# Attention by halves: when a head's second 256 queries may begin

## The chip, the cores and the metric

The kernel runs on one core of a Trainium2 chip. The metric is the time of one execution on the device, in microseconds (us). The core's engines work side by side, each through a list of its own, and wait for each other by semaphores: TensorE (PE, with its weight loads as PEld), VectorE (DVE), ScalarE (ACT), GpSimd (POOL) and SyncE (SP), which issues the DMA transfers.

## What is computed

One residual block over 1024 tokens of 1024 features, in float32. Cut to what matters:

```
h = x + 0.5 * g1 * swiglu(n1, w1, w3, w2)            # first FFN
proj = n2 @ w_in
y_rwkv = rwkv7_mixer(proj[..., :N_RWKV_COLS], ...)   # 8 heads, a recurrence
...
bias = rel_bias[:, rel_idx]                          # 8 heads of 64
scores = jnp.einsum('bhcqd,bhckd->bhcqk', q, k_band) * (HEAD_DIM ** -0.5)
scores = scores + bias[None, :, None]                # each 64 frames see themselves and 512 before
probs = jax.nn.softmax(scores, axis=-1)
out = jnp.einsum('bhcqk,bhckd->bhcqd', probs, v_band)
...
mixed = jnp.concatenate([y_rwkv, y_attn], axis=-1) @ w_out
h = h + g2 * mixed
h = h + 0.5 * g3 * swiglu(n3, ...)                   # second FFN
```

## The kernel before

The tokens are worked in two halves, A and B, of 512. Each half goes through first FFN, input projection, recurrence and attention, output projection and second FFN. The big products ("mm", or "mmb" where the result lies in one of the shared banks) keep float32 accuracy by splitting each operand into a high and a low part and multiplying three times: weights arrive as "wst", ScalarE makes the high part "whi" and VectorE the low part "wlo"; activations are "nh" and "nl", the FFN's hidden values "ah" and "al" (from "sw"), the mixed heads "mh" and "ml". Each such product has 128 rows of weights and streams 512 columns.

Everything is written as generators. A generator yields what it needs next: tiles that have to be ready, or the name of a pool in which a buffer has to be free. `drive` keeps a clock of estimated times for every engine and resumes the first task, in the order of priorities, whose needs the clock has ready; if there is none, it moves its clock to the earliest. So the program's order on every engine, fixed when the program is built, comes from these priorities and estimates. The big products come from one task of the lowest priority, `products`, and fill what the others leave. The FFN's two output stages of one token half can be interrupted by a projection only as `pick` allows: first FFN of A, projection of A, first FFN of B (which is begun before that projection and goes on behind it), output projection of A, projection of B, second FFN of A (into which the output projection of B is put as soon as the mixed heads of B are there), second FFN of B.

Attention has one pair of tasks for each of eight heads and each token half: `head_in` loads and splits keys, queries and values (K, QH, QL, V) and the bias, and `attention` does the rest, in two rounds of 256 queries (`for qp in range(2)`), each of two blocks of 128. For each block: scores S on TensorE (two products, QH and QL); VectorE adds the bias, writes E and its maximum; ScalarE takes the exponential and scales by the reciprocal sum; TensorE transposes E in blocks of 128 keys ("tr"); ScalarE copies the high part of the transposed probabilities ("pt") and VectorE subtracts to get the low part; TensorE multiplies both with the values ("yp"); ScalarE and VectorE add the two halves of yp into yT, which is stored when both rounds are done. There are 2 buffers for E, 6 in the pool "t2" (yT, pt, QH, QL and the loads), 2 for K and V, 1 for the bias, and 5 shared PSUM banks "b" (S, tr, yp, the recurrence's products and part of the big ones). A head's task starts when the task of the head before it has ended; so the next round's scores come behind the last yT of the round before.

The recurrence (`rwkv1`, `inverse`, `rwkv2`) runs at the same time. Its products are small ("px", "pu", "pz", "gb", "bt" and others); `inverse` is a long list of VectorE operations on "BKB" and "ln". "V" is the values' split.

Of the kernel before, what the change touches and what calls it, by code (L numbers as in the profile page):

```python
# [8 lines left out]
F32 = mybir.dt.float32  # L9
F32R = mybir.dt.float32r  # L10
AF = mybir.ActivationFunctionType
OP = mybir.AluOpType
# [4 lines left out]
P = 128  # L17
T = 1024
D = 1024
H = 512  # L20
# [8 lines left out]
NEG = -3.0e38  # L29
# [220 lines left out]
class Builder:  # L250
# [770 lines left out]
    def head_in(self, hf, hd, st):  # L1021
# [44 lines left out]
        yield vd  # L1066
        nc.scalar.activation(V[:, :, 0], vd, AF.Copy)
        yield V
        nc.vector.tensor_sub(V[:, :, 1], vd, V[:, :, 0].bitcast(F32))
        st["V"] = V  # L1070

    def attention(self, hf, hd, st):
        nc = self.nc
        p, h = hd // 2, hd % 2
        hs = slice(h * 64, h * 64 + 64)
        has = lambda k: lambda: self.clock.ready(st[k]) if k in st else NEVER
        yield has("QL"), has("bias")
        QH, QL, K, bias = (st[k] for k in ("QH", "QL", "K", "bias"))
        yield "t2"
        yT = self.t2("yT")  # L1080
        for qp in range(2):
            pr = []
            for i in range(2):
                b = 4 * hf + 2 * qp + i
                k0 = max(0, b - 4)
                n = (b - k0 + 1) * P
                q = (2 * qp + i) * P
                S = []

                m = n if n <= H else n // 2  # L1090
                for c0 in range(0, n, m):
                    yield QL, K, "b"
                    S.append((self.bank("S"), c0, m))
                    k = k0 * P + c0
                    self.mm(S[-1][0][:, 0:m], QH[:, q : q + P], K[:, k : k + m], start=True, stop=False)
                    self.mm(S[-1][0][:, 0:m], QL[:, q : q + P], K[:, k : k + m], start=False, stop=True)
                yield *(x[0] for x in S), "E"
                E = self.sm("E", [P, 640], 2)
                sm = self.sm("st", [P, 4], 4)
                for j, (x, c0, m) in enumerate(S):  # L1100
                    nc.vector.tensor_tensor_reduce(
                        out=E[:, c0 : c0 + m], in0=x[:, 0:m], in1=bias[:, 640 - n + c0 : 640 - n + c0 + m],
                        scale=1.0, scalar=NEG, op0=OP.add, op1=OP.max, accum_out=sm[:, 2 * j : 2 * j + 1],
                    )
                if n > H:
                    nc.vector.tensor_scalar(sm[:, 1:2], sm[:, 0:1], sm[:, 2:3], -1.0, OP.max, OP.mult)
                else:
                    nc.vector.tensor_scalar(sm[:, 1:2], sm[:, 0:1], -1.0, None, OP.mult)
                pr.append((b, k0, E, sm, n))
            if qp == 1:  # L1110
                self.free(K, QH, QL)
            for b, k0, E, sm, n in pr:
                yield sm
                nc.scalar.activation(E[:, 0:n], E[:, 0:n], AF.Exp, bias=sm[:, 1:2], accum_out=sm[:, 2:3])
            for b, k0, E, sm, n in pr:
                yield sm
                nc.vector.reciprocal(sm[:, 3:4], sm[:, 2:3])
            for b, k0, E, sm, n in pr:
                yield E, sm
                nc.scalar.activation(E[:, 0:n], E[:, 0:n], AF.Copy, scale=sm[:, 3:4])  # L1120
                self.free(sm)
            blocks = []
            for kb in range(pr[0][1], pr[1][0] + 1):
                blocks.append((kb, [i for i in range(2) if pr[i][1] <= kb <= pr[i][0]]))
            blocks.sort(key=lambda x: -len(x[1]))
            nb = len(blocks)
            trs, pts, yp = {}, {}, None
            span = lambda bi: slice(blocks[bi][1][0] * P, blocks[bi][1][-1] * P + P)
            for bi in range(nb + 2):
                if bi < nb:  # L1130
                    kb, use = blocks[bi]
                    yield *(pr[i][2] for i in use), "b"
                    trs[bi] = self.bank("tr", 2)
                    for i in use:
                        k0 = pr[i][1]
                        self.tp_(trs[bi][:, i * P : i * P + P], pr[i][2][:, (kb - k0) * P : (kb - k0 + 1) * P], self.ident)
                if bi == nb - 1:
                    self.free(pr[0][2], pr[1][2])
                if 1 <= bi <= nb:
                    yield pts[bi - 1]  # L1140
                    c = span(bi - 1)
                    nc.vector.tensor_sub(pts[bi - 1][:, 1, c], trs[bi - 1][:, c], pts[bi - 1][:, 0, c].bitcast(F32))
                if bi < nb:
                    yield trs[bi], "t2"
                    c = span(bi)
                    pts[bi] = self.t2("pt", [P, 2, 256], F32R)
                    nc.scalar.activation(pts[bi][:, 0, c], trs[bi][:, c], AF.Copy)
                if 1 <= bi <= nb:
                    yield pts[bi - 1], has("V"), *(["b"] if bi == 1 else [])
                    V = st["V"]  # L1150
                    if bi == 1:
                        yp = self.bank("yp", 2)
                    c = span(bi - 1)
                    lv = V[:, blocks[bi - 1][0]].rearrange("p a c -> p (a c)")
                    pt = pts.pop(bi - 1)
                    self.mm(yp[:, c], lv, pt[:, 0, c], start=bi == 1, stop=False, skip_group_check=True)
                    self.mm(yp[:, c], lv, pt[:, 1, c], start=False, stop=bi == nb, skip_group_check=True)
                    self.free(pt)
            q0 = qp * 256
            yield yp  # L1160
            nc.scalar.activation(yT[0:64, q0 : q0 + 256], yp[64:128, 0:256], AF.Copy)
            yield yT
            nc.vector.tensor_add(yT[0:64, q0 : q0 + 256], yT[0:64, q0 : q0 + 256], yp[0:64, 0:256])
# [588 lines left out]
```

## Time and profile before

| what | value |
|---|---|
| median of 3 runs | 2111.45 us (2110.54 to 2112.09) |
| the profiled execution, its own time | 2110.92 us |
| its span, from the first to the last instruction | 2109.0 us |
| TensorE busy | 2086.1 us, 99% of the span |
| VectorE busy | 1443.9 us, 68% |
| ScalarE busy | 946.7 us, 45% |
| GpSimd busy | 119.2 us, 6% |

The span is shorter than the execution's own time by what lies ahead of the first and behind the last instruction. Matrix products overlap each other in their records: each lasts longer than the distance to the next one's start, so TensorE's busy time says that it always has something in work, not how fast it starts the next. For that, read the starts in the timeline.

### The profile page before, as it was taken

To read this page: it belongs to the slowest core of one execution; us is meant where nothing else is said; L and a number is where in the kernel's file an instruction comes from. 1 tells how busy PE (TensorE), PEld (TensorE's weight loads), DVE (VectorE), ACT (ScalarE), POOL (GpSimd) and SP (SyncE) were. 2 spreads that over 40 slices of the span, in tenths; PEclk is the share of its full clock that TensorE was granted. 3 is DMA by queue.
4 is the path that set the end of the run, shared out by engine and by line. 5 is a ranking of instruction groups with operands and counts; after the bars stand their busy time and mean duration, and the time that the engine had idled before them with its cause. 6 is when DMAs were issued, how large, how long until landed. Compare 5 with 4: busy or idle time off the path is not lost.

```text
span 2109.0 us, 31735 instructions
## 1 busy us (share of the span) xinstructions
PE 2086.1 (99%) x10956; PEld 1715.0 (81%) x10956; DVE 1443.9 (68%) x2994; ACT 946.7 (45%) x1889; POOL 119.2 (6%) x162
## 2 busy tenths in 40 slices
PE   7999999999999999999999999999999999999999
PEld 4788888888878888888888888888888878888887
DVE  7877777654678788857764689688877664444444
ACT  4332224444654554354555654745465443322332
POOL 0000000011310010001011300010001000000000
PEclk9999999999999999999999999999999999999999
DMA  7766665434863434324654845344343554333332
GB/s 253 244 199 213 202 191 164 129 119 150 258 204 117 119 114 123 99 76 154 209 166 159 262 134 167 100 132 113 114 111 92 190 162 152 127 96 100 95 95 100
DMA packets 228928, 316.49 MB, mean 150 GB/s; under 512 B 55968, under 2 KB 95904, under 8 KB 228768
## 3 DMA queue, kind: packets, MB, share of 16 engines
q1 hardware_dynamic: 228768, 314.48, 48.3%
q8 instruction: 86, 1.41, 0.3%
q14 instruction: 74, 0.61, 0.1%
HBM read 279.78 MB, written 34.61 MB: 149 GB/s over the span
## 4 chain that ended last, share of the span: by engine, by line
PE 96%; DVE 2%; ACT 1%; DMA 1%; issue 0%; SPq 0%; DVEq 0%; ACTq 0%
PE mm L523 80%; PE mmb L523 4%; PE yp L523 2%; PE S L523 1%; PE tr L527 1%; PE gb L523 1%; PE cs L527 1%; PE pu L523 1%; PE pz L523 1%; PE px L523 1%; PE yb L523 1%; PE row L523 1%; PE first L523 0%; PE gate L523 0%; PE trq L527 0%
## 5 line engine op out<-in xcount | busy, mean ns | idle before, releaser
L176 ACT ACTIVATE whi<-wst 128x512 fp32r<-128x512 f32 (+2 forms) x692 | 423.6, 613 | 808.1 <-PE mm L523 680.1
L176 DVE TENSOR_TENSOR wlo<-wst,whi 128x512 fp32r<-128x512 f32 (+2 forms) x692 | 463.5, 673 | 347.5 <-ACT whi L176 332.4
L523 PE MATMUL mm<-nh,whi 128*128 128x512 f32 x1520 | 616.0, 405 | 0.3 <-ACT nh L176 0.3
L523 PE MATMUL mm<-nl,whi 128*128 128x512 f32 x1520 | 594.4, 391 | 1.9 <-DVE nl L176 1.7
L523 PE MATMUL mm<-nh,wlo 128*128 128x512 f32 x1520 | 593.9, 391 | 0.0
L523 PEld LDWEIGHTS mm<-nh,wlo 128*128 128x128 f32 x1520 | 285.7, 188 | 61.1
L523 PEld LDWEIGHTS mm<-nl,whi 128*128 128x128 f32 x1520 | 286.6, 189 | 53.3 <-DVE nl L176 3.5
L523 PEld LDWEIGHTS mm<-nh,whi 128*128 128x128 f32 x1520 | 286.3, 188 | 53.0 <-issue 1.2
L523 PE MATMUL mm<-ah,whi 128*128 128x512 f32 x651 | 261.4, 402 | 1.0 <-ACT ah L176 0.9
L523 PE MATMUL mm<-al,whi 128*128 128x512 f32 x651 | 254.4, 391 | 1.1 <-DVE al L176 1.0
L523 PE MATMUL mm<-ah,wlo 128*128 128x512 f32 x651 | 254.2, 390 | 0.0
L176 DVE SCALAR_TENSOR_TENSOR h<-mm,g,h 128x512 f32<-128x512 f32 x177 | 131.5, 746 | 86.2 <-PE mm L523 85.7
L523 PEld LDWEIGHTS mm<-ah,wlo 128*128 128x128 f32 x651 | 122.3, 188 | 25.9
L523 PEld LDWEIGHTS mm<-ah,whi 128*128 128x128 f32 x651 | 122.6, 188 | 25.0 <-ACT ah L176 1.7
L523 PEld LDWEIGHTS mm<-al,whi 128*128 128x128 f32 x651 | 122.7, 188 | 24.2 <-DVE al L176 2.0
L176 ACT ACTIVATE E<-E,st 128x640 f32<-128x640 f32 (+4 forms) x128 | 86.4, 689 | 24.4 <-DVE st L176 23.3
L176 DVE SCALAR_TENSOR_TENSOR acc<-wa,silc,acc 128x512 f32<-128x512 f32 (+1 forms) x133 | 89.6, 677 | 1.3 <-DMA wa<-in_w_ada 0.2
L176 DVE TENSOR_TENSOR sw<-sw,mm 128x512 f32<-128x512 f32 x85 | 58.5, 688 | 36.6 <-PE mm L523 33.9
L523 PE MATMUL mm<-whi,nh 128*128 128x512 f32 x192 | 76.9, 401 | 0.0
L523 PE MATMUL mm<-wlo,nh 128*128 128x512 f32 x192 | 75.0, 390 | 0.0
L523 PE MATMUL mm<-whi,nl 128*128 128x512 f32 x192 | 75.0, 390 | 0.0
L176 ACT ACTIVATE pt<-tr 128x256 fp32r<-128x256 f32 x144 | 49.3, 344 | 57.2 <-PE tr L527 55.7
(247 smaller groups left out, 2666.5 us busy)
## 6 DMA issues: line engine op xcount, KB each, us to landing
wst<-in_ffn_w SPq DMA_DIRECT2D x468, 256.0 KB, 2.8
wa<-in_w_ada SPq DMA_DIRECT2D x144, 256.0 KB, 4.1
wst<-in_w_v SPq DMA_DIRECT2D x64, 256.0 KB, 2.8
wst<-in_ffn_w SPq DMA_DIRECT2D x64, 192.0 KB, 2.4
wst<-in_w_t SPq DMA_DIRECT2D x40, 256.0 KB, 4.1
wst<-in_w_out SPq DMA_DIRECT2D x32, 256.0 KB, 3.0
kd<-kT SPq DMA_DIRECT2D x48, 128.0 KB, 3.6
bias<-in_bias SPq DMA_DIRECT2D x16, 320.0 KB, 4.1
```

Source lines behind the costliest of these rows:

```text
L176: return f(*args, **kw)
L523: self.nc.tensor.matmul(out, lhsT, rhs, start=start, stop=stop, **kw)
L527: self.nc.tensor.transpose(out, in_, ident)
```

## The change

`attention` is made a task for one round of 256 queries, so that there are 16 for a token half where there were 8. The second round's task may start when the first has issued its last transpose of E and given up its two E buffers (`self.done.add(free)`); the next head's first round likewise behind this head's second. It no longer waits for the round's products with the values and for yT. yT is taken from its pool when yp is done instead of when the head begins. `head_in` of a head still follows `head_in` of the head before. The whole of attention is done when all second rounds have ended. The body of a round is the same, one level further left:

```diff
-    def attention(self, hf, hd, st):
+    def attention(self, hf, hd, qp, st, free):
+
         nc = self.nc
...
         QH, QL, K, bias = (st[k] for k in ("QH", "QL", "K", "bias"))
-        yield "t2"
-        yT = self.t2("yT")
-        for qp in range(2):
-            pr = []
-            for i in range(2):
...
+        pr = []
+        for i in range(2):
...
+            if bi == nb - 1:
+                self.free(pr[0][2], pr[1][2])
+                self.done.add(free)
...
-            q0 = qp * 256
-            yield yp
...
+        q0 = qp * 256
+        if qp == 0:
+            yield yp, "t2"
+            yT = self.t2("yT")
+        else:
+            yield yp, has("y")
+            yT = st["y"]
...
+        if qp == 0:
+            st["y"] = yT
+            return
         self.free(V)
         yield yT
...
-            self.spawn(f"{name}h{h}", self.attention(hf, h, st), 4, before)
-            last, before = [f"{name}i{h}"], [f"{name}h{h}"]
-        self.spawn(name, self.late(lambda: iter(())), 4, before)
+            for qp in range(2):
+                e = f"{name}e{h}{qp}"
+                self.spawn(f"{name}h{h}{qp}", self.attention(hf, h, qp, st, e), 4, before)
+                before = [e]
+            last = [f"{name}i{h}"]
+        self.spawn(name, self.late(lambda: iter(())), 4, [f"{name}h{h}1" for h in range(8)])
```

Every engine has the same instructions before and after, in another order. The number behind a name tells one buffer's use from the next; numbers differ between the two programs.

TensorE, the end of a head's first round in token half B, while the projection of B fills the gaps. Before:

```order
L523 MATMUL yp_12274<-pt_12326,V_12128 128x256 x2
L527 MATMUL tr_12350<-ident,E_12179 128x128
L523 MATMUL mm_12289<-nh_10756,whi_12220 128x512
L523 MATMUL mm_12289<-nl_10717,whi_12220 128x512
L523 MATMUL mm_12289<-nh_10756,wlo_12221 128x512
L523 MATMUL yp_12274<-pt_12346,V_12128 128x128 x2
L523 MATMUL mm_12289<-nh_10779,whi_12220 128x512
L523 MATMUL mm_12289<-nl_10776,whi_12220 128x512
L523 MATMUL mm_12289<-nh_10779,wlo_12221 128x512
L523 MATMUL yp_12274<-pt_12356,V_12128 128x128 x2
```

The last transpose makes pt_12356; three projection products, a pair of value products and three more projection products stand between the two. Of the same place, now:

```order
L523 MATMUL yp_12228<-pt_12285,V_12128 128x256 x2
L527 MATMUL tr_12306<-ident,E_12147 128x128
L523 MATMUL S_12309<-K_11908,QH_12007 128x320
L523 MATMUL S_12309<-K_11908,QL_12021 128x320
L523 MATMUL S_12317<-K_11908,QH_12007 128x320
L523 MATMUL S_12317<-K_11908,QL_12021 128x320
L523 MATMUL yp_12228<-pt_12302,V_12128 128x128 x2
L523 MATMUL S_12328<-K_11908,QH_12007 128x320
L523 MATMUL S_12328<-K_11908,QL_12021 128x320
L523 MATMUL yp_12228<-pt_12315,V_12128 128x128 x2
```

The last transpose makes pt_12315; six score products of the second round have moved to the place of the projection products, which follow later.

TensorE, in the second FFN of A, where the down products reach the last hidden values of a group of columns. Before:

```order
L523 MATMUL mm_15650<-ah_15413,whi_15524 128x512
L523 MATMUL mm_15650<-al_15414,whi_15524 128x512
L523 MATMUL mm_15650<-ah_15413,wlo_15525 128x512
L523 MATMUL yp_15654<-pt_15666,V_15460 128x256 x2
L527 MATMUL tr_15681<-ident,E_15501 128x128
L523 MATMUL mm_15597<-ah_15593,whi_15441 128x512
L523 MATMUL mm_15597<-al_15594,whi_15441 128x512
L523 MATMUL mm_15597<-ah_15593,wlo_15442 128x512
```

ah_15593 and al_15594 are the last hidden values; most of a round of attention lies among the 27 products of the hidden values before them. The same place now:

```order
L523 MATMUL mmb_15843<-al_15654,whi_15771 128x512
L523 MATMUL mmb_15843<-ah_15653,wlo_15772 128x512
L527 MATMUL tr_15865<-ident,E_15719 128x128
L527 MATMUL tr_15865<-ident,E_15774 128x128
L527 MATMUL tr_15870<-ident,E_15719 128x128
L527 MATMUL tr_15870<-ident,E_15774 128x128
L523 MATMUL mm_15811<-ah_15805,whi_15694 128x512
L523 MATMUL mm_15811<-al_15806,whi_15694 128x512
```

The round there is at its first transposes; only these four stand between the 27 products and the last hidden values, ah_15805 and al_15806.

VectorE at the same two places, from the gate's second operation "sw" to the low half "al". Before:

```order
L176 TENSOR_TENSOR sw_15595<-sw_15595,mm_15468 128x512
L176 TENSOR_REDUCE bon_15606<-cs_15607 128x8
L176 TENSOR_TENSOR al_15594<-sw_15595,ah_15593 128x512
L176 TENSOR_TENSOR pt_15639<-tr_15632,pt_15639 128x256
L176 TENSOR_TENSOR pt_15648<-tr_15641,pt_15648 128x256
```

One reduction of the recurrence stands between "sw" and "al". Now:

```order
L176 TENSOR_TENSOR sw_15807<-sw_15807,mm_15741 128x512
L176 TENSOR_TENSOR wlo_15816<-wst_15674,whi_15815 128x512
L176 RECIPROCAL st_15720<-st_15720 128x1
L176 TENSOR_TENSOR V_15792<-vd_15793,V_15792 128x8x64
L176 RECIPROCAL st_15775<-st_15775 128x1
L176 TENSOR_TENSOR ln_15681<-BKB_15631 64x234
L176 TENSOR_TENSOR BKB_15631<-BKB_15631,ln_15681 64x13x18
L176 TENSOR_TENSOR ln_15681<-BKB_15631 64x238
L176 TENSOR_TENSOR BKB_15631<-BKB_15631,ln_15681 64x14x17
L176 TENSOR_TENSOR ln_15681<-BKB_15631 64x240
L176 TENSOR_TENSOR BKB_15631<-BKB_15631,ln_15681 64x15x16
L176 TENSOR_TENSOR al_15806<-sw_15807,ah_15805 128x512
```

A weight's low half, the split of V, two reciprocals and six steps of the block inverse stand there now.

## Rows read from the trace of the kernel before

**Rows 1.** The page, span and TensorE: busy us (share) xinstructions.

```profile
span 2109.0 us, 31735 instructions
PE 2086.1 (99%) x10956; PEld 1715.0 (81%) x10956; DVE 1443.9 (68%) x2994; ACT 946.7 (45%) x1889; POOL 119.2 (6%) x162
```

**Rows 2.** TensorE's two longest waits: us in total, times, longest.

```profile
PE cs L527 <- DVE ssq L176: 13.2, 1, 13.2
PE mm L523 <- DVE nl L176: 1.7, 2, 1.3
```

**Rows 3.** Busy time by stretch: PE, PEld, DVE, ACT, POOL, clock, DMA.

```profile
522.00:1736.00 1214.00, 1211.01 (x7048) 998.64 (x7047) 910.75 (x2106) 635.77 (x1364) 99.01 (x125) 1.00 0.48 146
...
1140.00:1230.00 90.00, 89.95 (x458) 74.65 (x457) 60.27 (x134) 55.26 (x111) 20.88 (x24) 1.00 0.74 224
...
614.00:674.00 60.00, 60.00 (x319) 49.31 (x318) 47.60 (x115) 27.01 (x58) 0.29 (x2) 1.00 0.52 159
674.00:704.00 30.00, 30.00 (x141) 24.96 (x140) 27.45 (x66) 13.39 (x27) 1.38 (x5) 1.00 0.39 109
1740.00:2109.00 369.00, 365.25 (x1612) 302.39 (x1610) 167.01 (x254) 108.80 (x180) 0.00 (x0) 1.00 0.35 109
```

**Rows 4.** Timeline of TensorE behind a pair of transposes: start us, duration us.

```profile
1475.97 0.48 PE L523 MATMUL mm<-ah,whi 128*128 128x512 f32 x1
1476.29 0.39 PE L523 MATMUL mm<-al,whi 128*128 128x512 f32 x1
1476.52 0.39 PE L523 MATMUL mm<-ah,wlo 128*128 128x512 f32 x1
```

**Rows 5.** Timeline of TensorE, two score products in a row.

```profile
1461.11 0.31 PE L523 MATMUL S<-K,QH 128*128 128x320 f32 x1
1461.25 0.31 PE L523 MATMUL S<-K,QL 128*128 128x320 f32 x1
```

**Rows 6.** Timeline at the first pair of order fences, VectorE free.

```profile
1194.42 0.47 PE L523 MATMUL mm<-nh,whi 128*128 128x512 f32 x1
...
1195.02 0.29 DVE L176 TENSOR_TENSOR pt<-tr,pt 128x128 fp32r<-128x128 f32 x1 [0.36 <-ACT pt L176]
...
1196.11 0.33 PE L523 MATMUL yp<-pt,V 128*128 128x128 f32 x2
...
1196.28 0.44 PE L523 MATMUL mm<-nh,whi 128*128 128x512 f32 x1
```

**Rows 7.** Timeline, earlier in the same round, VectorE held.

```profile
1185.96 1.78 DVE L176 TENSOR_TENSOR V<-vd,V 128x512 fp32r<-128x512 f32 x1
...
1187.66 0.68 DVE L176 TENSOR_TENSOR wlo<-wst,whi 128x512 fp32r<-128x512 f32 x1
...
1188.26 0.41 DVE L176 TENSOR_TENSOR pt<-tr,pt 128x256 fp32r<-128x256 f32 x1
1188.40 0.72 PE L523 MATMUL yp<-pt,V 128*128 128x256 f32 x2
...
1188.73 0.19 PEld L523 LDWEIGHTS yp<-pt,V 128*128 128x128 f32 x1 [0.37 <-DVE pt L176]
```

**Rows 8.** A step of the block inverse: xcount, busy us, mean ns.

```profile
L176 DVE TENSOR_TENSOR BKB<-BKB,ln 64x240 f32<-64x240 f32 x8 | 3.2, 400 | 0.3
```

**Rows 9.** Timeline of TensorE at the last group of A's second FFN.

```profile
1731.84 0.39 PE L523 MATMUL mmb<-ah,wlo 128*128 128x512 f32 x1
1733.17 0.51 PE L523 MATMUL mm<-ah,whi 128*128 128x512 f32 x1 [0.94 <-ACT ah L176]
```

**Rows 10.** VectorE from 516 us; then E, st and pt alone from 725 us.

```profile
516.00:725.00 209.00, 154.21 (x380) 1.00 0.58 176
...
725.00:857.00 132.00, 5.56 (x27) 3.62 (x27) 3.84 (x8) 10.55 (x26) 1.00 0.38 112
725.00:857.00 132.00, 3.02 (x25) 10.55 (x26) 1.00 0.38 112
725.00:857.00 132.00, 6.70 (x32) 5.57 (x32) 5.90 (x16) 5.49 (x16) 1.00 0.38 112
```

More of the change, by code (lines that the diff above doesn't have):

```diff
@@ L1078, in attention @@
         QH, QL, K, bias = (st[k] for k in ("QH", "QL", "K", "bias"))
-        yield "t2"
-        yT = self.t2("yT")
-        for qp in range(2):
-            pr = []
-            for i in range(2):
[L1084 to L1158, printed above, removed]
-            q0 = qp * 256
-            yield yp
-            nc.scalar.activation(yT[0:64, q0 : q0 + 256], yp[64:128, 0:256], AF.Copy)
-            yield yT
-            nc.vector.tensor_add(yT[0:64, q0 : q0 + 256], yT[0:64, q0 : q0 + 256], yp[0:64, 0:256])
@@ new lines, in attention @@
+        pr = []
+        for i in range(2):
+            b = 4 * hf + 2 * qp + i
+            k0 = max(0, b - 4)
+            n = (b - k0 + 1) * P
+            q = (2 * qp + i) * P
+            S = []
+            m = n if n <= H else n // 2
+            for c0 in range(0, n, m):
+                yield QL, K, "b"
+                S.append((self.bank("S"), c0, m))
+                k = k0 * P + c0
+                self.mm(S[-1][0][:, 0:m], QH[:, q : q + P], K[:, k : k + m], start=True, stop=False)
+                self.mm(S[-1][0][:, 0:m], QL[:, q : q + P], K[:, k : k + m], start=False, stop=True)
+            yield *(x[0] for x in S), "E"
+            E = self.sm("E", [P, 640], 2)
+            sm = self.sm("st", [P, 4], 4)
+            for j, (x, c0, m) in enumerate(S):
+                nc.vector.tensor_tensor_reduce(
+                    out=E[:, c0 : c0 + m], in0=x[:, 0:m], in1=bias[:, 640 - n + c0 : 640 - n + c0 + m],
+                    scale=1.0, scalar=NEG, op0=OP.add, op1=OP.max, accum_out=sm[:, 2 * j : 2 * j + 1],
+                )
+            if n > H:
+                nc.vector.tensor_scalar(sm[:, 1:2], sm[:, 0:1], sm[:, 2:3], -1.0, OP.max, OP.mult)
+            else:
+                nc.vector.tensor_scalar(sm[:, 1:2], sm[:, 0:1], -1.0, None, OP.mult)
+            pr.append((b, k0, E, sm, n))
@@ new lines, in attention @@
+        if qp == 1:
+            self.free(K, QH, QL)
+        for b, k0, E, sm, n in pr:
+            yield sm
+            nc.scalar.activation(E[:, 0:n], E[:, 0:n], AF.Exp, bias=sm[:, 1:2], accum_out=sm[:, 2:3])
+        for b, k0, E, sm, n in pr:
+            yield sm
+            nc.vector.reciprocal(sm[:, 3:4], sm[:, 2:3])
+        for b, k0, E, sm, n in pr:
+            yield E, sm
+            nc.scalar.activation(E[:, 0:n], E[:, 0:n], AF.Copy, scale=sm[:, 3:4])
+            self.free(sm)
@@ new lines, in attention @@
+        blocks = []
+        for kb in range(pr[0][1], pr[1][0] + 1):
+            blocks.append((kb, [i for i in range(2) if pr[i][1] <= kb <= pr[i][0]]))
+        blocks.sort(key=lambda x: -len(x[1]))
+        nb = len(blocks)
+        trs, pts, yp = {}, {}, None
+        span = lambda bi: slice(blocks[bi][1][0] * P, blocks[bi][1][-1] * P + P)
+        for bi in range(nb + 2):
+            if bi < nb:
+                kb, use = blocks[bi]
+                yield *(pr[i][2] for i in use), "b"
+                trs[bi] = self.bank("tr", 2)
+                for i in use:
+                    k0 = pr[i][1]
+                    self.tp_(trs[bi][:, i * P : i * P + P], pr[i][2][:, (kb - k0) * P : (kb - k0 + 1) * P], self.ident)
+            if bi == nb - 1:
+                self.free(pr[0][2], pr[1][2])
+                self.done.add(free)
+            if 1 <= bi <= nb:
+                yield pts[bi - 1]
+                c = span(bi - 1)
+                nc.vector.tensor_sub(pts[bi - 1][:, 1, c], trs[bi - 1][:, c], pts[bi - 1][:, 0, c].bitcast(F32))
+            if bi < nb:
+                yield trs[bi], "t2"
+                c = span(bi)
+                pts[bi] = self.t2("pt", [P, 2, 256], F32R)
+                nc.scalar.activation(pts[bi][:, 0, c], trs[bi][:, c], AF.Copy)
+            if 1 <= bi <= nb:
+                yield pts[bi - 1], has("V"), *(["b"] if bi == 1 else [])
+                V = st["V"]
+                if bi == 1:
+                    yp = self.bank("yp", 2)
+                c = span(bi - 1)
+                lv = V[:, blocks[bi - 1][0]].rearrange("p a c -> p (a c)")
+                pt = pts.pop(bi - 1)
+                self.mm(yp[:, c], lv, pt[:, 0, c], start=bi == 1, stop=False, skip_group_check=True)
+                self.mm(yp[:, c], lv, pt[:, 1, c], start=False, stop=bi == nb, skip_group_check=True)
+                self.free(pt)
@@ L1164, in attention @@
+        q0 = qp * 256
+        if qp == 0:
+            yield yp, "t2"
+            yT = self.t2("yT")
+        else:
+            yield yp, has("y")
+            yT = st["y"]
+        nc.scalar.activation(yT[0:64, q0 : q0 + 256], yp[64:128, 0:256], AF.Copy)
+        yield yT
+        nc.vector.tensor_add(yT[0:64, q0 : q0 + 256], yT[0:64, q0 : q0 + 256], yp[0:64, 0:256])
+        if qp == 0:
+            st["y"] = yT
+            return
         self.free(V)
```

## The prediction

> **What bounds the kernel now.** I read the page's busy times first, then TensorE's waits, then its stretches, then single stretches of its timeline. TensorE is busy 99% of the span [rows 1]. What it waits for is short: 13.2 us once, at the start, and behind that no single wait above 1.3 us [rows 2]. In the stretch from 522 to 1736 us, which holds all attention and ends where the two programs are the same again, it is idle for 1214 - 1211.01 = 2.99 us, at a granted clock of 1.00, the upper level of 2.4 GHz [rows 3]. Products of 512 columns start 0.23 us apart although one takes 0.39 us (1476.29 and 1476.52) [rows 4]: a start that is late by less than 0.16 us doesn't show as idle time. So the kernel ends when TensorE has got through its list. The change adds and takes away no instruction there; it can only shorten or lengthen the distances between starts.
>
> **What moves.** Counted in products of 512 columns, attention of the first token half runs from product 2058 to 3180 now, and to 2787 in the new order; that of the second half from 4320 to 5943, and to 5760. It was the last thing that the second output projection waited for, so that projection's first product moves from 6025 to 5857. But what stood behind attention was never empty: the second FFN of the first token half fills TensorE until the projection comes, and it now stands behind instead of ahead. 168 products by 0.23 us is 39 us of work that changes places, not 39 us of gain.
>
> **Term 1, the breaks.** Behind a pair of transposes the second product starts 0.32 us after the first (1475.97 and 1476.29), where it is 0.23 otherwise [rows 4]. So the return to products costs at most 0.09 us. The return from transposes to products stands 201 times in the order now and 175 times in the new one; the return from the recurrence's small products stands 84 and 104 times. Six fewer by 0.09 us is 0.5 us of gain, by nothing is 0. The share of the 0.09 that a longer run of transposes saves isn't in these rows; I take the whole: -0.5 us.
>
> **Term 2, a half's probabilities.** In the first pair of order fences six score products of the next half stand where six plain ones stood. A score product of 320 columns passes in 0.14 to 0.15 us [rows 5], a pair of value products of 128 columns in 0.17 us (1196.11 to 1196.28) [rows 6]. So between the last transpose and the value products that need it the new order leaves 6 x 0.145 + 0.17 = 1.04 us, where the same place takes 1.69 us now (from 1194.42, the product right behind the transpose, to 1196.11) [rows 6]. That is enough if VectorE is free: its subtraction ends 0.89 us after 1194.42 (1195.02 + 0.29) [rows 6]. It isn't enough if something lies ahead on VectorE. [Rows 7] show that, at a place with the same cover: V's subtraction holds VectorE from 1185.96 for 1.78 us, a half weight follows for 0.68 us, the probabilities' subtraction comes at 1188.26 and ends at 1188.67, and the second value product starts at 1188.73, 0.33 us behind the first at 1188.40, where a pair of them takes 0.17 us for both: a stall of about 0.2 us. I walked through all 144 such places of the new order with the distances of the trace: ten have less cover than the 1.70 us that is the usual floor now, at 0.92, 1.03, 1.04, 1.27, 1.33, 1.33, 1.46, 1.46, 1.62 and 1.63 us. Together they lack 3.9 us. The upper end is that each stalls by all that it lacks: 3.9 us. The lower end is that VectorE is free each time: then only the wide ones at 0.92 and 1.04 us lack something, about 0.2 us (a subtraction of 256 columns takes 0.41 us instead of 0.29 [rows 6, 7]). Eight of the ten stand where the order now has reached 1150 to 1210 us; from 1140 to 1230 VectorE is busy 60.27 of 90 us [rows 3], 67%, so neither end is likely. The cover there is longer than the bare 0.89 us in eight of ten; I take nearer to the lower end, +1.2 us. Nothing queues behind the waiting product but TensorE's own list, so each stall is paid in full.
>
> The Trainium skill says in "TensorE: Matmul & The Clock Gate", section "Architectural detail: the array is 16x 32x32, not 1x 128x128", that VectorE's and ScalarE's queues are strictly first in, first out, while TensorE may load weights ahead. By that rule anything a second half puts on VectorE early delays what stands behind it in the list, and term 2 would be its upper end, +3.9 us, and the sum 2.7 us more. [Rows 7] agree: the subtraction of 1188.26 had its input and waited its turn.
>
> **Term 3, the FFN's hidden values.** In the second pair of fences the FFN's last up product hands over to the down product. Now 27 down products of other hidden columns and most of a half's transposes and value products lie between; in the new order only the 27 and four transposes: 27 x 0.23 = 6.2 us and a little. The third pair shows what VectorE has to do in that time: three operations of 128x512 ("sw", "wlo", "al"), 3 x 0.68, V at up to 1.78 [rows 7], and six steps of the block inverse at 0.40 [rows 8], 6.2 us. The two just meet. If VectorE comes to it late, TensorE stalls, as it did at the last such place now: from 1731.84 to 1733.17, 1.33 us where 0.23 would do [rows 9]. Bounds 0 and 1.1 us, by that row; I take the middle, +0.5 us. That stall itself falls together with the norm of the second token half, which shares VectorE with the last hidden values; with the projection earlier the norm meets the group before, with the same work: 0, bounds -1.1 and +1.1.
>
> **Costs at nothing.** The tile for a half's result is asked for later, keys and queries are freed earlier, the next head's loads (SP's queue) start earlier; their cover is the whole preceding half, and none of TensorE's waits, of which [rows 2] has the longest, is on a head's load or a weight. What comes earlier also comes more densely: the five of sixteen halves that ran after 725 us carry 3.84 + 3.02 + 5.90 = 12.8 us of VectorE's work, and VectorE is busy 154.21 of the 209 us before that [rows 10]: 167 of 209, 80%, where 27.45 of 30 us (92%, at 674) pass without TensorE waiting [rows 3].
>
> **Sum.** -0.5 + 1.2 + 0.5 + 0 = +1.2 us on the profiled execution's 2110.92 us (span 2109.0 and 1.9 us around it): 2112.1 us. The median of the runs, 2111.45 us, is 0.5 us above that execution: 2112.6 us.
>
> **Rivals.** (a) *VectorE becomes the bound* while the first half of the tokens has its attention: slower. In [rows 10] 12.8 us move; spread over 209 us they fit. Were all of them to fall into the 60 us from 614, which the new order makes the densest, VectorE, at 47.60 of 60 us there [rows 3], would need 60.4 us and its waits on top. At the 92% that is its highest share over 30 us, 60.4 us of work takes 65.7 us: TensorE loses 5.7 us, and with the +1.2 us of the sum the time is 2118.3 us. It decides from the point where over 7.6 of the 12.8 us fall there (55.2 of 60 us being 92%). The four weight blocks that are kept ahead speak against it. Chance 0.15, with terms 2 and 3 at their upper ends.
> (b) *What stalls now goes.* All 2.99 us of idle time in the stretch, and about the same again in starts that are late without showing, came from attention and the norm being late, and all of it goes: 2112.6 - 1.2 - 0.5 - 4 = 2106.9 us. Faster. Against it: the longest of those waits, at 1733, is on an FFN's hidden value and not on attention [rows 9]. Chance 0.05.
> (c) *Nothing moves in time* although attention ends earlier, terms 2 and 3 at their lower ends: 2111.2 us, inside the same verdict as the forecast.
>
> "Perfetto Trace Analysis" of the Trainium skill, section "Identifying the Most-Contended Engine", says that TensorE's headroom isn't read from busy products but from the share of weight loads. By that rule 17.7% of the stretch would be free (998.64 of 1214 us of loads), and a denser attention could fill it. The trace doesn't bear this out: in the last 369 us, plain products with no attention, the share is the same, 302.39 of 369 or 82% [rows 3], at 0.23 us a product; it is part of (b)'s chance.
>
> **How the numbers follow.** The forecast and (c) have 0.80. About 0.2% (4.2 us) is what measuring this kernel can tell from no change: below 2107.2 faster, above 2115.7 slower. So faster 0.05, same 0.80, slower 0.15. The range: the lower end is (c) with all of term 1 and the stall at 1733 gone, 2109 us; the upper end reaches to (a), 2118 us, with both terms at their upper ends (+2.7 and +0.6) on the way at 2115.9 us. About 0.1 lies on either side.
>
> **What would show it.** TensorE's waits after: some on "pt" by VectorE, each under 0.8 us, in the stretch from 1140 to 1230 us, which now has 89.95 of 90 us busy [rows 3]; one on "al" or "ah" near 1480 us; idle time in 522 to 1736 of 3 to 5 us; the last value product near 1600 us, the projection's first about 39 us earlier. Wrong would be: waits on "wlo" around 614 to 674 us (then it is (a)), or an idle time there below 1 us (then (b)).

## The result, and the profile after

The changed kernel takes 2126.26 us (2124.95 to 2130.5), the kernel before 2110.99 in the same runs: a ratio of 1.0071, interval 1.0059 to 1.0083. It is 15 us slower, where 2112.6 us and a range up to 2118 were forecast. The profiled execution is the slowest of the four (2130.5 us), so what is counted in its trace below adds up to more than 15 us. Its page:

```profile
span 2128.7 us, 31740 instructions
PE 2092.4 (98%) x10956; PEld 1716.8 (81%) x10956; DVE 1448.6 (68%) x2994; ACT 947.5 (45%) x1889; POOL 120.1 (6%) x162
```

TensorE's waits in it (us in total, times, longest):

```profile
PE cs L527 <- DVE ssq L176: 13.4, 1, 13.4
PE yp L523 <- DVE pt L176: 5.6, 7, 1.9
PE mm L523 <- DVE al L176: 4.3, 4, 1.8
PE mm L523 <- DVE nl L176: 1.8, 2, 1.5
PE tr L527 <- ACT E L176: 1.5, 3, 0.9
PE pu L523 <- ACT Xd L176: 1.0, 2, 0.6
PE mm L523 <- ACT ah L176: 0.9, 1, 0.9
PE cs L527 <- ACT sq L176: 0.9, 1, 0.9
...
```

Against [rows 2] the waits on "pt" and "E" are new, and those on "al" have grown; in the kernel before they were:

```profile
PE mm L523 <- DVE al L176: 1.0, 2, 0.8
```

The engines' totals hardly differ from [rows 1]. Next the stretches, of the changed kernel (us of busy time: PE, PEld, DVE, ACT, POOL; then clock, DMA share, GB/s); the first runs from where the two orders part to where they are the same again:

```profile
523.50:1734.43 1210.93, 1194.88 (x6955) 981.99 (x6953) 906.42 (x2091) 629.87 (x1351) 99.89 (x125) 1.00 0.48 145
...
522.00:614.00 92.00, 87.69 (x422) 70.40 (x420) 64.91 (x152) 60.64 (x137) 21.50 (x27) 0.98 0.71 219
614.00:674.00 60.00, 57.96 (x348) 46.73 (x347) 50.29 (x130) 29.87 (x68) 0.88 (x6) 1.00 0.53 161
...
1140.00:1230.00 90.00, 86.86 (x434) 72.08 (x433) 57.62 (x139) 55.48 (x114) 21.24 (x24) 1.00 0.71 225
```

and the first of these for the kernel before, between the same two points of TensorE's list:

```profile
521.99:1712.91 1190.92, 1189.09 (x6954) 981.02 (x6953) 891.51 (x2075) 623.49 (x1342) 99.01 (x125) 1.00 0.48 146
```

The same list takes 20.0 us longer. Of the whole difference of the two spans (19.7 us) another 1.5 us lie ahead of this stretch, where the lists are the same and the clock differs (61 to 65 us: 0.61 here, 1.00 in the kernel before), and 1.8 us come back behind it, where the kernel before has its stall at 1733 [rows 9].

TensorE is idle for 16.05 us in the stretch instead of 1.83: 14.2 us. The other 5.8 us are in longer busy time. Part of that is the clock. The granted clock of a stretch is a mean over its two levels, 1.00 (2.4 GHz) and 0.50 (1.2 GHz); it fell at two of the waits:

```profile
578.00:582.00 4.00, 1.81 (x9) 1.42 (x8) 3.88 (x9) 3.57 (x8) 1.20 (x1) 0.84 0.36 133
582.00:586.00 4.00, 4.00 (x16) 3.21 (x16) 0.59 (x4) 1.00 (x3) 3.71 (x7) 0.73 0.75 199
...
1704.00:1708.00 4.00, 4.00 (x13) 3.13 (x12) 3.80 (x7) 1.69 (x4) 0.00 (x0) 0.61 0.18 56
```

At the lower level products start 0.43 us apart (582.55, 582.98, 583.41) instead of 0.23. The eight starts from 1704.23 to 1707.19 come 1.6 us later by it, and the other stretch is about as long: some 3 us, an estimate. What is left, some 2.8 us, I take to be starts that are late without showing as idle time; that is not shown by itself.

The largest single wait is at 581.11, the product with the second part of a "pt". TensorE, and below it VectorE's list over the same time:

```profile
573.92 0.38 PE L527 MATMUL tr<-ident,E 128*128 128x128 f32 x2
...
577.83 0.36 PE L523 MATMUL yp<-pt,V 128*128 128x256 f32 x1
578.52 0.39 PE L523 MATMUL yp<-pt,V 128*128 128x256 f32 x1 [0.33 <-DVE pt L176]
578.75 0.38 PE L527 MATMUL tr<-ident,E 128*128 128x128 f32 x2
578.89 0.36 PE L523 MATMUL yp<-pt,V 128*128 128x256 f32 x1
581.11 0.58 PE L523 MATMUL yp<-pt,V 128*128 128x256 f32 x1 [1.85 <-DVE pt L176]
...
574.02 1.75 DVE L176 TENSOR_TENSOR so<-so,sh 128x512 f32<-128x512 f32 x1
...
578.07 0.40 DVE L176 TENSOR_TENSOR pt<-tr,pt 128x256 fp32r<-128x256 f32 x1
578.50 0.69 DVE L176 TENSOR_TENSOR K<-kd,K 64x512 fp32r<-64x512 f32 x1
579.23 0.69 DVE L176 TENSOR_TENSOR wlo<-wst,whi 128x512 fp32r<-128x512 f32 x1
579.83 0.68 DVE L176 TENSOR_REDUCE rk<-cs 128x8 f32<-128x512 f32 x1
580.55 0.17 DVE L176 TENSOR_SCALAR rk<-rk 128x8 f32<-128x8 f32 x1
580.63 0.42 DVE L176 TENSOR_TENSOR pt<-tr,pt 128x256 fp32r<-128x256 f32 x1
```

VectorE isn't idle for a moment from 574.02 on. The "pt" that TensorE needs is the last of these operations, behind four of the recurrence, another "pt", the next head's K, a weight half and two more of the recurrence. ScalarE's copy for this "pt" is late too: its transposes start at 573.92, and it runs at 577.27, behind an operation ("sq") that had itself waited 1.83 us for VectorE's "so". The wait on "al" at 639.52 (1.77 us) and the one at 1502.01 (0.94 us) look alike: VectorE is busy 11.66 of the 12 us from 628 and 7.55 of the 8 us from 1494.

### The profile page after: what moved, and what is told of

Read it like the earlier page. It is cut to its first block, busy times and chain, and to the rows that moved or that the text cites. A ratio compares the mean times of both kernels' runs of the same rounds, so it can differ in the third digit from the quotient of the medians.

```text
span 2128.7 us, 31740 instructions
## 1 busy us (share of the span) xinstructions
PE 2092.4 (98%) x10956; PEld 1716.8 (81%) x10956; DVE 1448.6 (68%) x2994; ACT 947.5 (45%) x1889; POOL 120.1 (6%) x162
## 4 chain that ended last, share of the span: by engine, by line
PE 91%; DVE 4%; DMA 2%; issue 1%; ACT 1%; SPq 0%; POOL 0%; DVEq 0%; ACTq 0%; POOLq 0%
PE mm L523 76%; PE mmb L523 4%; PE yp L523 1%; PE S L523 1%; PE tr L527 1%; PE px L523 1%; PE gb L523 1%; PE cs L527 1%; DVE wlo L176 1%; PE pu L523 1%; PE pz L523 1%; PE row L523 1%; PE first L523 1%; PE yb L523 0%; SPq L176 0%
## 5 line engine op out<-in xcount | busy, mean ns | idle before, releaser
L523 PE MATMUL mm<-al,whi 128*128 128x512 f32 x662 | 259.2, 391 | 4.3 <-DVE al L176 4.3
L523 PE MATMUL mm<-ah,wlo 128*128 128x512 f32 x662 | 258.6, 391 | 0.0
```

What stands on the lines that cost most here:

```text
L523: self.nc.tensor.matmul(out, lhsT, rhs, start=start, stop=stop, **kw)
```

## The experiments

The first theory was that VectorE's work falls too dense. Each run's ratio is to the kernel before on the same chip; the two numbers behind it in brackets are its 95% interval.

**Which half of the tokens.** In `spawn_attention`, the early start in A alone, and (with `hf == 1`) in B alone:

```diff
-                before = [e]
+                before = [e] if hf == 0 else [f"{name}h{h}{qp}"]
```

> Only the first token half (A) begins a round of queries once the round before has its last transpose of E; half B keeps the old rule, so TensorE's order up to the middle of the program is that of the changed kernel and behind it that of the kernel before. Theory, VectorE comes late in bursts: in the two profiles the stretch of A in which the orders differ lost 9.4 us (521.97 to 977.37 us before, 523.48 to 988.23 after), some 2 us of it at the lower clock right behind a wait; so 2117 to 2121 us, with waits on pt near 578 and on al near 639 us as in the changed kernel. Rival, the loss comes from one half alone or from the projection that moves (half B): 2111 us within 2 us.

> Only the second token half (B) begins its rounds early. Theory: the other half of the loss, about 9 us in the profile of the changed kernel (10.7 us late at the start of B's attention, 19.7 at the end): 2116 to 2120 us, with waits on pt near 1185 to 1215, on al near 1490 and on ah and al at the norm of B near 1690 us. Rival, the loss comes from half A: 2111 us within 2 us. If the two halves do not add up to about +15 us, something outside both has a share.

Measured: A 2119.77 us (1.0036, 1.0022 to 1.005), B 2118.72 us (1.0032, 1.0022 to 1.0042). That is 7.8 and 6.7 us, together 14.5. Both are as expected: the loss is made in both halves, and the two shares add up. A's share can't come from the projection that comes earlier behind B, since in that run it doesn't; how much of B's share does isn't told apart.

**VectorE cheaper, nothing moved.** `clock`, which keeps the estimated times, still books each operation as before, so all lists are unchanged; only what VectorE executes is lighter, which leaves out the low parts and the recurrence's products and sums:

```diff
+            if self.name == "vector" and op in ("tensor_sub", "tensor_add", "tensor_mul", "tensor_tensor", "scalar_tensor_tensor"):
+                o, x, y = args[0], args[1], args[3 if op == "scalar_tensor_tensor" else 2]
+                if not any(z.name in self.clock.psum for z in (o, x, y)):
+                    z = y if op == "tensor_sub" and y.dtype == F32 and list(y.shape) == list(o.shape) else x
+                    return self.eng.tensor_scalar(o, z, 1.0, None, OP.mult)
```

> Control: the kernel before, all engines in the same order, but each VectorE operation with two operands in SBUF is issued as a multiplication of one of them by 1 (the low parts, the recurrence's products and the sums are left out by that), which takes 0.42 us where a 128x512 one takes 0.69. TensorE's list is unchanged. Both theories: 2108 to 2111 us, since VectorE holds up TensorE for less than 3 us there.

> The changed kernel, all engines in the same order, with the same cheaper VectorE operations (same parts left out). Theory, VectorE's queue is late: the 11 us of VectorE's work ahead of the late al near 639 us lose about 3 us, more than the wait of 1.9 us, so most waits go and the difference to the lean kernel before falls from 15 us to at most 4 us. Rival, it is TensorE's own order (breaks between kinds of products), ScalarE or the transfers: the difference stays at 12 us or more.

Measured: 2101.26 and 2108.53 us (0.9949 and 0.9984 of the kernel before; 0.9936 to 0.9961 and 0.9975 to 0.9993). The difference is 7.3 us, half of the 15: more than the theory's 4, less than the rival's 12. The kernel before itself missed its expectation, 2101 instead of 2108 to 2111 us: in its profile 4.1 us are gained in the first 75 us, where TensorE's one long wait, on "ssq", falls from 13.2 to 9.2 us, and the rest later, most of it while attention runs. In the lean changed kernel the waits on "al" are gone. Of what stayed the longest stands behind these rows, VectorE's and GpSimd's in the lean changed kernel:

```profile
1178.55 1.30 POOL L181 TENSOR_TENSOR pv<-pv,muv 128x512 f32<-128x512 f32 x1
...
1178.90 1.23 DVE L180 TENSOR_SCALAR V<-V 128x512 fp32r<-128x512 f32 x1 [3.81 <-ACT V L181]
...
1179.93 1.32 POOL L181 TENSOR_TENSOR pv<-pv,pv 128x512 f32<-128x512 f32 x1
...
1180.05 1.48 DVE L180 TENSOR_SCALAR wlo<-whi 128x512 fp32r<-128x512 f32 x1
...
1181.46 0.41 DVE L181 TENSOR_TENSOR pt<-tr,pt 128x256 fp32r<-128x256 f32 x1
...
1181.92 0.39 PE L528 MATMUL yp<-pt,V 128*128 128x256 f32 x1 [1.29 <-DVE pt L181]
```

Beside GpSimd's "pv" operations that take 0.42 and 0.43 us elsewhere in this run take 1.23 and 1.48. So GpSimd was taken away next.

**GpSimd's part.** Its operations on "pv" are issued on 8 of 512 columns, alone and together with the edit above:

```diff
+            if self.name == "gpsimd" and op == "tensor_tensor" and OP.pow not in args and width(args[0]) == H and len(args[0].shape) == 2:
+                args = [x[:, 0:8] if is_ap(x) else x for x in args]
```

> Control: the kernel before in its own order, with GpSimd's 24 operations on pv issued on 8 columns of 512 (the shift of the recurrence's values is left out by that). In its profile VectorE's operations that lie beside a GpSimd operation last 10.6 us longer than the same ones elsewhere, but TensorE waits for none of them: 2110 to 2112 us by every theory.

> The changed kernel in its own order, with GpSimd's operations on pv issued on 8 columns (same part left out). Theory, part of VectorE's lateness comes from GpSimd: a low part beside pv takes 1.59 to 1.77 us instead of 0.68, and such operations stand ahead of the late pt near 578 (2.0 us longer), 1196 (1.1), 1202 (0.9) and 1222 us (1.1); without them 4 to 5 us of waits go and the lower clock behind the first: the difference to the same edit of the kernel before is 8 to 10 us instead of 14 to 15. Rival, VectorE's own list alone makes it late: the difference stays at 13 us or more.

> Control: the kernel before with both edits, VectorE's operations on two operands in SBUF issued as a multiplication of one by 1 and GpSimd's on pv on 8 columns (the low parts, the recurrence's products and sums, and the shift of the values are left out). About as the lean kernel before alone, 2099 to 2102 us.

> The changed kernel with both edits (same parts left out), TensorE's list unchanged. In the lean changed kernel 3.8 us of waits on pt and a stretch at the lower clock remained, each behind a VectorE operation of 1.2 to 1.5 us beside pv. Theory, VectorE's own work and GpSimd's slowing of it are the whole cause: the difference to the control falls to at most 2.5 us. Rival, something besides VectorE (TensorE's order, ScalarE, transfers) has a share: it stays at 5 us or more.

Measured: alone 2111.31 and 2126.25 us (0.9997, 0.9988 to 1.0006, and 1.0066, 1.0053 to 1.0078), a difference of 14.9: nothing came back. With both edits 2101.67 and 2106.03 us (0.9954, 0.994 to 0.9967, and 0.9974, 0.9965 to 0.9984), a difference of 4.4. My expectation of 8 to 10 us for the first difference was wrong, and the 4.4 us lie between what theory (at most 2.5) and rival (5 or more) gave. With "pv" alone out of the way the waits on "pt" fell from 5.6 to 3.9 us, but those on "E" by ScalarE rose from 1.5 to 2.6, the longest of them at 599.68:

```profile
599.68 0.33 PE L529 MATMUL tr<-ident,E 128*128 128x128 f32 x1 [2.11 <-ACT E L178]
```

There E's scaling stands in ScalarE's list behind the next head's QH, whose load is late. In the changed kernel it is the same:

```profile
600.98 0.63 ACT L176 ACTIVATE QH<-qd 128x512 fp32r<-128x512 f32 x1 [1.51 <-DMA qd<-qT]
```

So what one engine gave back another took. The 4.4 us are explained by neither edit.

**Which start, and two ways to hold it back.** In turn: only a head's second round early (`if qp == 0`), only the next head's first round early (`if qp == 1`); scores held until VectorE is free on the estimated clock; value products no sooner than 0.7 us behind the moment at which their task asks for them on that clock ("0.7 us later" from here on):

```diff
+                before = [e] if qp == 0 else [f"{name}h{h}{qp}"]
...
-                yield QL, K, "b"
+                yield QL, K, "b", self.idle("vector") if i == 0 else 0.0
...
-                yield pts[bi - 1], has("V"), *(["b"] if bi == 1 else [])
+                yield pts[bi - 1], has("V"), 0.7, *(["b"] if bi == 1 else [])
```

> Only a head's second round begins early, behind the last transpose of its first; the next head still waits until the second round has ended. Theory, VectorE's list gets too dense by the work that the overlap brings forward: the second round brings its two evictions of scores, the next head in addition its splits of K, QL and V, so this half of the overlap costs less than half of the 15 us: 2113 to 2118 us. Rival, the value products lose their cover by any overlap alike: two thirds or more of it, 2121 us or more.

> Only the next head's first round begins early, behind the last transpose of the second round of the head before; a head's second round waits until its first has ended. Theory: the larger part of the cost, with the head loads' splits brought forward and waits on al: 2117 to 2123 us. Rival: a third of it or less, 2116 us or less.

> The changed kernel, but a round's first scores are issued only when the estimated clock has VectorE free (or less than 0.8 us ahead of TensorE). Theory, bursts on VectorE: rounds begin early only where VectorE has room, most waits on pt and al go: 2110 to 2116 us. Rival, the waits come from TensorE's list, which has no products between transposes and values, and from head loads that come late to ScalarE: 2120 us or more.

> The changed kernel, but the products with the values may be issued only 0.7 us later on the estimated clock, so other work of TensorE moves in between. Theory: the waits on pt (5.6 us in the changed kernel) fall below 2.5 us, those on al stay: 2118 to 2123 us. Rival, where TensorE waits it has no other work to put there, and VectorE stays as late: 2124 us or more.

Measured: 2115.98 us (1.0022, 1.0013 to 1.003), 2118.94 (1.0032, 1.0019 to 1.0044), 2126.03 (1.0064, 1.005 to 1.0078) and 2112.49 (1.0005, 0.9995 to 1.0014). The first two are as expected. The last two speak against the first theory. Holding rounds back for VectorE gives nothing, though that is a weak test: VectorE has 62.01 and 50.22 us of work in the two stretches below, little less than in the changed kernel. Postponing a product on TensorE gives 14 us; its time lies below both expectations. In that fast variant VectorE is denser than in the changed kernel in the same stretches, and TensorE is not idle in the second:

```profile
522.00:614.00 92.00, 88.95 (x460) 71.28 (x460) 68.26 (x156) 59.81 (x134) 22.94 (x28) 1.00 0.70 219
614.00:674.00 60.00, 60.00 (x327) 49.59 (x328) 52.90 (x138) 30.65 (x69) 0.58 (x4) 1.00 0.57 161
```

Two of the fast variant's waits, the first on "pt", the second on "al":

```profile
PE yp L523 <- DVE pt L176: 0.9, 1, 0.9
...
PE mm L523 <- DVE al L176: 0.7, 1, 0.7
```

So VectorE does 52.90 us of work in 60 without a wait of TensorE here, and 50.29 in the changed kernel with 2.04 us of TensorE's idle time. Nor is it how fast attention goes: the last scores stand at product 5811, 5805, 5799 and 5802 in the four, within 12 products, and their times lie 13.5 us apart. (These numbers count TensorE's products of 512 columns, as the prediction does; the last scores stand at 5646 in the changed kernel and at 5898 in the kernel before.) What the last edit changes directly is the work between an operand's last transpose and the product that needs it, its cover; every list shifts with it.

**Dose and control.** The second theory: a wait is the time by which VectorE's list ahead of a needed operand is longer than its cover, TensorE's work up to the product. The same 0.7 us in the kernel before; 0.35 us in the changed kernel; the FFN's "al" taken as ready 1.0 us later; 0.7 us for both:

```diff
+        self.clock.wr[al.name] += 1.0
```

> Control: the kernel before, with the products with the values issued 0.7 us later on the estimated clock. Theory, cover: TensorE has no wait on pt there, so nothing is to be had; 2109 to 2113 us. Rival, the later value products make any order faster: 2098 to 2102 us, as far below the kernel before as the same edit took off the changed one.

> The changed kernel with the value products only 0.35 us later; attention ends nearly as early as in the changed kernel (last scores at product 5709, where it is 5646 there, 5802 with 0.7 us and 5898 before). Theory, cover: about half of the loss goes, 2116 to 2122 us. Rival, time follows how early attention ends: 2122 us or more.

> The changed kernel, the estimated clock takes the FFN's low hidden values al as ready 1.0 us later, so that their products come later; value products as in the changed kernel. Theory, cover: the waits on al (4.3 us) go, those on pt stay (5.6 us): 2119 to 2123 us. Rival, the waits on al are only passed on to the next operand: 2124 us or more.

> The changed kernel with the value products 0.7 us later and al taken as ready 0.7 us later. Theory, cover: as with the value products alone or up to 2 us less, since one wait on al of 0.7 us was left: 2109 to 2113 us. Rival: no gain, or the norm's work is pushed back, 2114 us or more.

Measured: the control 2133.2 us (1.0104, 1.009 to 1.0118), 0.35 us 2118.22 (1.0034, 1.0021 to 1.0048), "al" 2125.1 (1.0069, 1.0057 to 1.0082), both 2115.09 (1.0016, 1.0008 to 1.0025). At 0.35 us about half of the loss goes, as expected; the value products wait 3.5 us for "pt" there (1.9 of them for ScalarE's high part), where they wait 5.6 without delay and 0.9 at 0.7 us. "Both" lies above the theory's 2109 to 2113 us and above 0.7 us alone. The control missed both expectations, for a reason of its own. Its waits from 1690 to 1800 us:

```profile
PE mm L523 <- ACT mh L176: 4.2, 3, 1.7
PE rb L527 <- ACT wide L176: 2.8, 1, 2.8
PE cs L527 <- DVE ssq L176: 2.3, 1, 2.3
PE mm L523 <- ACT nh L176: 2.3, 1, 2.3
...
```

With value products later and rounds not earlier, the last scores stand at product 6051. The second FFN, which fills TensorE till then, runs out, and the projection waits for the mixed heads; the clock falls with the waits (0.57 from 1709 to 1717 us and 0.53 from 1757 to 1768). So attention's earlier end is worth something where attention is late, and nothing in the kernel before, where it isn't. "al" shows that a wait removed isn't time removed, as the rival had it: those waits fell from 4.3 to 1.3 us, the time by 1.2 us against the result above, within the scatter of its runs.

**Further along the scale**, 1.0 and 1.4 us:

> The changed kernel with the value products 1.0 us later on the estimated clock (last scores at product 5778; 5802 with 0.7 us). Theory, cover: nearly nothing is left to remove, 2109 to 2113 us, at the kernel before; since TensorE's list is the same length, not below 2108. Rival, the early rounds pay once they are covered: below 2108 us.

> The changed kernel with the value products 1.4 us later (last scores at product 5889, as late as in the kernel before at 5898). Theory: 2109 to 2114 us, the early start used up by the delay and the projection still in time. Rival, attention gets too slow as in the control: waits on mh or ml by the second output projection and 2116 us or more.

Measured: 2128.54 us (1.0078, 1.0065 to 1.0092) and 2126.58 (1.007, 1.0058 to 1.0083), both far above what I expected. The value products' waits on VectorE's "pt" are 0.9 us and none; the time went into single new ones, with the lower clock at them (0.52 from 1498 to 1505 us, 0.53 from 1742 to 1753). The longest at 1.0 us:

```profile
1499.60 0.80 PE L523 MATMUL mm<-ah,wlo 128*128 128x512 f32 x1 [4.47 <-DVE wlo L176]
```

and at 1.4 us, TensorE's row and ScalarE's:

```profile
1744.27 0.79 PE L523 MATMUL mm<-ah,whi 128*128 128x512 f32 x1 [4.62 <-ACT ah L176]
...
1743.60 0.61 ACT L176 ACTIVATE ah<-sw 128x512 fp32r<-128x512 f32 x1
```

Both are of the kind shown at 581: "wlo" is last in a VectorE list that has been full for 8 us, and "ah" stands in ScalarE's list behind an "nh" that itself waits for VectorE's "nv". So the cover theory holds for the operand whose cover is changed, and doesn't give the total, since each edit reorders all lists and makes other operands meet. That 0.7 us, of the four delays, brought the time back to the kernel before is in part luck: the totals at 0.35, 0.7, 1.0 and 1.4 us follow no line.

**What all runs share.** Fourteen of the profiles are of kernels that do all of the work (before, changed and twelve variants); their spans go from 2109.0 to 2131.9 us. Take from each TensorE's idle time between 60 us and its last product, and half of its time at the lower clock, and 2103 to 2106.5 us are left. So all but some 3 us of each loss is idle time and the clock; which operand is waited for changes from order to order.

## Why the prediction was wrong

**The bound** was read rightly. TensorE does the same products, and the whole loss is in the distances between their starts.

**Term 1**, the breaks (-0.5 us), can't be told apart from the rest; at that size it is no matter for the miss.

**Term 2**, a round's probabilities (+1.2 us, at most 3.9), is the step that failed: the waits on "pt" are 5.6 us, where the kernel before has none. The mechanism is the one measured: the second value product waits for VectorE's "pt". The size was wrong because of how the places were chosen. I took as candidates those with less cover than the 1.70 us that is the usual floor in the kernel before, and found ten, eight of them at 1150 to 1210 us. Of the 5.6 us 2.1 lie there (1196.34, 1199.39 and 1203.68), 3.5 at places that weren't on the list. The floor is no property of the chip; it is what the lists of that order left. What counts is VectorE's list ahead of the operand. The largest wait, at 581.11, is on transposes that start at 573.92, with unbroken work of TensorE behind them until 576.56. That alone is 2.6 us, more than the floor, so the walk left it out. VectorE's list ahead of that "pt", from 574.02 to 580.63, takes 6.6 us. In 1140 to 1230 us, which I did name, the idle time is 3.14 us, toward the upper end of 3.9, and its longest single wait is 1.6 us instead of under 0.8.

The FIFO rule of the Trainium skill ("TensorE: Matmul & The Clock Gate", section "Architectural detail: the array is 16x 32x32, not 1x 128x128"), beside which the prediction set the upper end of this term, agrees with the waits looked at here: the subtraction at 580.63 had its input from ScalarE at 577.63 (577.27 and 0.36 us) and ran behind all that stood ahead of it. What was missing was the walk through the list itself.

**Term 3**, the FFN's hidden values (+0.5 us, at most 1.1): the wait near 1480 is there, 0.94 us on "al" at 1502, near the upper end. But I priced one place. The same hand-over at the first FFN's group boundary (639.52) cost 1.77 us, and all waits on "al" 4.3 us, against 1.0 in the kernel before: 3.3 us, three times the bound.

**The stall at 1733** [rows 9], taken as 0 with bounds of 1.1 us, got longer: there the changed kernel starts "ah" at 1701.66 and "al" at 1702.97, where the product ahead had started at 1700.39. That is 2.6 us for two steps of 0.23, where the kernel before took 2.1 (1731.84 to 1733.90), and the lower clock follows.

**Costs at nothing.** Three were not nothing. The next head's loads come earlier, and where they are late, ScalarE's E waits behind them (600.98 above; 1.5 us of waits on "E"). Small waits on the recurrence's operands and on "sw" had no term: "sw" 0.7, "RA" 1.0, and 0.5 more each on "Xd" and "sq". And the clock stood in no term, since it was 1.00 in every stretch read [rows 3]; here it cost some 3 us in the profiled execution.

**Rivals.** (a) was nearest in sign and size (2118.3 us) and wrong in its measure: VectorE isn't the bound of the 60 us (50.29 us busy, not 55.2), and there is no wait on "wlo" there. (b) is refuted: of 13 other orders of the same instructions (the changed kernel and twelve of the variants) none is faster than the kernel before. (c) is near what one variant came to (0.7 us, 2112.49 us), and two longer delays didn't. Two sums are off by themselves and don't bear on the miss: in (b) 2.99 us and about the same again are 6 us, not 4, and (c) without the stall of 1.1 us is 2110 us, not the 2109 of the range's lower end.

**What would show it**, as the prediction said: idle time of 3 to 5 us in 522 to 1736; it is 1214 - 1197.95 = 16 us. The last value product, expected near 1600 us, starts at 1619.2. The projection's first product was to come 39 us earlier: it starts at 1641.2 instead of 1661.7, 20.5 us earlier, the 39 less what was lost on the way.

**What stays open.** With both edits, VectorE's and GpSimd's, 4.4 us remain. Its profile still has waits on "pt" (2.0 us) and "E" (1.5 us), and from 522 to 1736 us TensorE is idle 3.6 us longer in it than in the kernel before with the same edits (1208.65 and 1212.29 us busy); which engine's list is behind them wasn't settled. Why the early starts worsen cover in both token halves by about the same is not shown either, nor why 0.7 us of delay is better than 1.0.

## What to carry to other kernels

In a program whose engines run fixed lists and whose bound engine is busy 99%, a reorder is priced operand by operand: for each product that needs another engine's result, the time of that engine's whole list ahead of the result against the bound engine's work up to the product. That says where waits will be; it gave no total here, because every edit made other operands meet. A busy share over 60 us doesn't show it (52.90 us without idle time, 50.29 with 2.04), and neither does a floor of cover taken from the old order. Ending a stream earlier was worth nothing here while TensorE had other work to fill with; before costing what such a reorder does, ask whether anything waits for that stream now.

## What was not expected of the hardware

The same waits of TensorE lowered the clock in one execution and not in another. In the profile of the changed kernel it fell at waits of 0.86, 0.33 and 1.85 us (577 to 581 us; the rows for 578 to 586 are above). In that of the variant with the early start in A alone, whose list is the same there, the waits are 0.84, 0.33 and 1.85 us, and the clock stayed at its upper level:

```profile
578.00:582.00 4.00, 1.83 (x10) 1.50 (x11) 3.67 (x8) 3.36 (x7) 1.41 (x1) 1.00 0.36 136
582.00:586.00 4.00, 4.00 (x22) 3.40 (x21) 1.95 (x10) 2.41 (x7) 3.71 (x7) 1.00 0.69 199
```

Single waits did both as well: at the hand-over near 639 us a wait of 1.77 us left it at 1.00 (638 to 642 us), and with "pv" on 8 columns a wait of 1.46 us at the same hand-over went with 0.60 over the same 4 us. Each fall cost some 1.5 us on top of its waits, by the estimate from the starts above. So a part of a single profile's time belongs to the execution and not to the order.

VectorE's operations last longer beside GpSimd's: a low part of 128x512 that takes 0.68 us took 1.56 to 1.77 beside "pv", and in the lean kernel one of 0.43 us took 1.48. With "pv" on 8 columns the low parts above 0.9 us went from seven to one in the changed kernel's list, so GpSimd's operation is the cause. That this cost nothing in the full kernels (14.9 us of difference without it) shows how little a slow operation says about the end.
